# Full-array products for the state step, the key transposes and the low-rank terms, S5 outputs sorted by form, and shared raw weight buffers, in a hybrid trunk layer

## Chip, cores and metric

One Trainium2 chip, of which the kernel uses one core. The metric is device time in microseconds for one execution; the median of three runs stands for a kernel. Lower is better.

## The reference

One layer of a streaming trunk over 2128 tokens (64 of a running stream, then 16 meta tokens and 2048 of a new stream), width 1024, all in float32:

```
x  = layer_norm(x)
P  = x @ w_in                        # 1024 x 11144, columns shared out among branches and gates
y_b = branch_b(P) * silu(gate_b(P))  # b = rwkv7 (12 heads of 64), s5 (32 groups), mlstm (4 heads of 192)
m  = sum_b sigmoid(P_merge_b + b_merge_b) * (y_b @ w_br_b)
out = layer_norm(DN_ALPHA * x + m @ w_out)
```

What the change touches is mostly the rwkv7 branch. Each head keeps a 64x64 state S, and per token

```
S = S * w_t + (S @ -kk_t) (kk_t * a_t)^T + v_t k_t^T;   y_t = S @ r_t
```

where w_t and a_t come from two low-rank terms (64 columns of P times a 64 x 768 matrix each). The s5 branch is a complex diagonal recurrence with 16 channels per group. The final states of both streams are outputs too.

## The kernel before, in words

**Blocks.** The tokens go through in five blocks of 336, 448, 448, 448 and 448 columns (blocks 1 to 5 below; the first has b.first in the code). Activations lie channels on partitions, tokens along the row. A block's normalised input x stands in sixteen tiles xh0 to xh7 and xl0 to xl7: x is split into a high part (float32r) and the rest, and so is each weight. A projection of 128 columns of P (proj, L435; mm3, L427) is 24 products of 128x128 weights with a whole block of columns: high x high, high x low, low x high for eight slices of the 1024. The tiles of x have one buffer each, so a block's can be loaded (load_x, L379) only when the block before has made its last product from them.

**Weights.** In block 1 the weights come raw: split_w (L392) loads 128x512 into a raw tile, ACT copies it to the high part (L403), POOL subtracts for the low part (L404), and both parts are stored to DRAM (L409) for the later blocks, which load them ready split (L423). The table WBUF gives the numbers of buffers: three raw and four each of high and low for projections ("w"), two and two for the merge gates ("g").

**Order.** Three generators, one per branch, are mixed by weights (mix, L1449; rw_block, ml_block, s5_stream); then gate_pass (L1493) adds the block's 24 merge gates, each a projection into the PSUM tile f, behind all of the block's other work. After block 5 follow the branch outputs and the final projection (merge_pass, L1503; its products are L1556). A planner turns this program into an order per engine: it simulates a timeline and prefers what comes earlier in the program, except where high_priority says otherwise. So the gates serve as fill. All weight loads, and most other DMAs, are issued by SP's queue.

**rwkv7, one head pair at a time** (6 pairs per block). Tokens are cut into slots of 64: 6 in block 1, 7 in the others, 34 in all; two heads lie on the two halves of the partitions. rw_front (L512) makes the operands; its low-rank terms (lmm, L527 to L530) are one 128x128 product and one with 64 rows on half the array. Products of the keys with AQ are L578. rw_prep (L628) inverts the triangular part and builds per slot the transition: it transposes AQ (L625), writes an identity into AQ[:, :, 0] (POOL, L679), transposes the keys BK of each head by itself (L689), multiplies (L684, L697, L705), and adds the result to AQ (L706). rw_back (L715) runs over the slots: two products of 64x64 per slot, one for each head (called at L739, issued at L723), and one DVE operation (L741) give the next state; then come the outputs. Tiles such as XV, AR and Tt have one buffer, AQ and AT two.

**S5.** s5_block (L1310), four channel groups per block. For each of four q one weight tile of 128x512 is loaded from s5wo, then two 128x128 products from U (L1368) and eight 64x64 products from H (L1375) add into two PSUM tiles.

A float32 product appears in the trace as two records of its line, a transpose or a float32r product as one. The lines that matter, before:

```
389  WBUF = {"w": (3, 4),
530      PE.matmul(p[:, :R], lora[q, 2, :], x[q], start=False, stop=True)
689          PE.transpose(p[h][:, c, :], bk[h][:, c, :], ident[hs[h], hs[h]])
706      V.tensor_tensor(AQ[:, c0:c0 + n], AQ[:, c0:c0 + n], p[:, :n], ALU.add)
739          mm(pc[hs[h]], AQ[hs[h], c, 0, :], Ss[hs[h]], True, True)
741      V.scalar_tensor_tensor(Ss, pc, Wc[:, c:c + 1], Ss, ALU.mult, ALU.add)
```

Of the kernel before, what the change touches and what calls it, by code (L numbers as in the profile page):

```python
# [83 lines left out]
def tile_trunk(ctx: ExitStack, tc: tile.TileContext, I, O, dbg=None, parts=("rw", "s5", "ml", "mg")):  # L84
# [286 lines left out]
    G.memset(Uin, 0.0)  # L371
    Tt = pt(c1, (128, NSL, 64), "Tt")
    G.memset(Tt, 0.0)
    id2 = pt(c1, (128, 64), "id2")
    for h in range(2):
        V.tensor_copy(id2[64 * h:64 * h + 64], ident[64 * h:64 * h + 64, 64 * h:64 * h + 64])
# [15 lines left out]
    def split_w(pool, src, kt, M, tag="w", keep=None):  # L392
        if keep is not None:
            wsp_d[keep] = pt(dram, (2, 2, 128, 4, 128), f"wsp{keep}")
        nr, nh = WBUF[tag]
        hi, lo = [], []
        for k in range(0, kt, 4):
            n = min(4, kt - k)
            h = pt(pool, (128, 4, 128), tag + "hi", F32R, bufs=nh)
            l = pt(pool, (128, 4, 128), tag + "lo", F32R, bufs=nh)  # L400
            raw = pt(pool, (128, 4, 128), tag + "raw", bufs=nr)
            nc.sync.dma_start(raw[:, :n, :M], src[:, k:k + n])
            S.copy(h[:, :n, :M], raw[:, :n, :M])  # L403
            G.tensor_tensor(l[:, :n, :M], raw[:, :n, :M], h.bitcast(F32)[:, :n, :M], ALU.subtract)  # L404
            hi += [h[:, m, :M] for m in range(n)]
            lo += [l[:, m, :M] for m in range(n)]
            if keep is not None:
                for j, t in enumerate((h, l)):
                    nc.sync.dma_start(wsp_d[keep][k // 4, j], t.bitcast(F32))  # L409
        return hi, lo  # L410
# [78 lines left out]
            V.tensor_tensor(t[l, :b.R], xs[h, :b.R], t.bitcast(F32)[h, :b.R], ALU.subtract)  # L489
        return xw, xa  # L490

    lora_d = pt(dram, (NHP, 128, 384), "lora")

    def lora_setup():
        raw = flat("X", 2 * RWW)
        hl = flat("va", 2 * RWW, F32R)
        r3, h3 = (t.rearrange("p (n c) -> p n c", c=RWW) for t in (raw, hl))
        for j, w in enumerate(("rw_w2", "rw_a2")):
            for a in range(2):
                nc.sync.dma_start(r3[64 * a:64 * a + 64, j], I[w][0])  # L500
        S.copy(h3, r3)
        l = flat("NK", 770, F32R)[:, :RWW]
        for j in range(2):
            q = slice(64 * j, 64 * j + 64)
            V.tensor_tensor(l[q], r3[q, j], h3.bitcast(F32)[q, j], ALU.subtract)
        v = lora_d.rearrange("n p (j c) -> p j n c", j=3)
        f = lambda t: t.bitcast(F32).rearrange("p (n c) -> p n c", c=128)
        for j in range(2):
            nc.sync.dma_start(v[:, j], f(h3[:, j]))
        nc.sync.dma_start(v[:, 2], f(l))  # L510

    def rw_front(b, hp, xwa, cx):  # L512
        R, nc_ = b.R, b.nslot
# [7 lines left out]
        kk = pt(rp, (128, RMAX), "kk")  # L521
        V.scalar_tensor_tensor(kk[:, :R], kx[:, :R], pcol("rw_kk", hp), rn[:, :R], ALU.mult, ALU.mult)
        yield
        lora = pt(rp, (128, 3, 128), "lora", F32R)
        nc.sync.dma_start(lora.bitcast(F32).rearrange("p j c -> p (j c)"), lora_d[hp])

        def lmm(p, j):  # L527
            x, q = xwa[j][:, :R], hs[j]
            PE.matmul(p[:, :R], lora[:, j, :], x, start=True, stop=False)
            PE.matmul(p[:, :R], lora[q, 2, :], x[q], start=False, stop=True)  # L530

        pw = psum((128, 512), "tr")
        lmm(pw, 0)
# [77 lines left out]
        for j in range(31):  # L611
# [3 lines left out]
            V.tensor_tensor(t3, Uin[:, j:j + 1, j + 1:32].to_broadcast((128, m, n)),  # L615
                            Z[:, 0:m, j:j + 1].to_broadcast((128, m, n)), ALU.mult)
            V.tensor_tensor(Z[:, 0:m, j + 1:32], Z[:, 0:m, j + 1:32], t3, ALU.add)  # L617
        cx.update(AT=AT, AQ=AQ, Z=Z, ni=ni, bk=bk, Wc=Wc, vx=vx, rx=rx, sg=sg, R=R, nc_=nc_, hs=hs)
        yield

    def pair_transposes(nc_, src):
# [4 lines left out]
        return p  # L626

    def rw_prep(b, hp, cx):  # L628
        AT, AQ, Z, ni, bk, Wc, vx, rx, R, nc_, hs = (
            cx[k] for k in ("AT", "AQ", "Z", "ni", "bk", "Wc", "vx", "rx", "R", "nc_", "hs"))  # L630
        Zd = pt(dram, (8, 4, 32, 32), "Zd", bufs=2)
        for g in range(4):
            QQ.dma_start(
# [41 lines left out]
        for q in range(2):  # L675
            n = (nc_ + 1 - q) // 2
            S.copy(AR[hs[0], q:nc_:2, 0, :], p[hs[q], :n, 0:64])
            V.tensor_copy(AR[hs[1], q:nc_:2, 0, :], p[hs[q], :n, 64:128])
        G.tensor_copy(AQ[:, :nc_, 0, :], id2[:, None, :].to_broadcast((128, nc_, 64)))  # L679
        p = psum((128, 8, 64), "tr")  # L680
        for c in range(nc_):
            for h in range(2):
                o = hs[1 - h]
                PE.matmul(p[hs[h], c, :], AT[o, c, h, 0:64], XV[o, c, h, :], start=True, stop=True)  # L684
        S.copy(AR[:, :nc_, 1, :], p[:, :nc_])
        p = [psum((128, 8, 64), "tr") for _ in range(2)]
        for c in range(nc_):
            for h in range(2):
                PE.transpose(p[h][:, c, :], bk[h][:, c, :], ident[hs[h], hs[h]])  # L689
        for h in range(2):  # L690
            S.copy(AT[:, :nc_, h, 0:64], p[h][:, :nc_])
        for c0 in range(0, nc_, 4):
            n = min(4, nc_ - c0)
            p = psum((128, 4, 2, 64), "tr")
# [5 lines left out]
        for c0 in range(0, nc_, 4):  # L700
            n = min(4, nc_ - c0)
            p = psum((128, 4, 2, 64), "tr")
            for c in range(n):
                for h in range(2):
                    PE.matmul(p[hs[h], c], PX[hs[h], c0 + c, 0, :], AT[hs[h], c0 + c, h, :], start=True, stop=True)  # L705
            V.tensor_tensor(AQ[:, c0:c0 + n], AQ[:, c0:c0 + n], p[:, :n], ALU.add)  # L706
        Hw = pt(rp, (128, NSL, 64), "Hw", bufs=1)
        p = psum((128, 8, 64), "tr")
        for c in range(nc_):
# [5 lines left out]
    def rw_back(b, hp, cx):  # L715
# [14 lines left out]
        for c in range(nc_):  # L730
            with tc.high_priority(offset=HPO):
                if b.first and c == 0:
                    Ss = state_in(hp)
                elif b.first and c == 1:
                    Ss = pt(rp, (128, 64), "Ss", bufs=2)
                    G.memset(Ss, 0.0)
                S0.append(Ss)
                for h in range(2):
                    mm(pc[hs[h]], AQ[hs[h], c, 0, :], Ss[hs[h]], True, True)  # L739
                Ss = Hw[:, c, :]  # L740
                V.scalar_tensor_tensor(Ss, pc, Wc[:, c:c + 1], Ss, ALU.mult, ALU.add)  # L741
# [568 lines left out]
    def s5_block(b, u_d, y_d):  # L1310
# [3 lines left out]
        for i in range(4):  # L1314
# [45 lines left out]
            yield  # L1360
            p = [psum((128, 4, NCM), "o") for _ in range(2)]
            prev = [None, None]
            for q in range(4):
                w = cut(w5(), 0, (128, 4, 128))
                nc.sync.dma_start(w, s5wo_d[4 * i + q])
                m = []
                for g in range(2):
                    m.append((g, PE.matmul(p[g][:, q, :NC], w[:, g, :], U[:, 2 * q + g], start=True, stop=False,  # L1368
                                           skip_group_check=True)))
                for ri in range(2):  # L1370
                    for a in range(2):
                        for g in range(2):
                            r = slice(64 * g, 64 * g + 64)
                            t = slice(64 * (a ^ g), 64 * (a ^ g) + 64)
                            m.append((g, PE.matmul(p[g][t, q, :NC], w[r, 2 + ri, t], H[r, q, ri, 0:NC], start=False,  # L1375
                                                   stop=ri == 1, skip_group_check=True)))
                for g, x in m:
                    if prev[g] is not None:
                        issue_after(x, prev[g])
                    prev[g] = x  # L1380
            yS = cut(sB(), 0, (128, 8, NC))
            for g in range(2):
                S.copy(yS.rearrange("p (q g) c -> p g q c", g=2)[:, g], p[g][:, :, :NC])
# [362 lines left out]
```

## Time and profile before

| | |
|---|---|
| runs shown | 4168.24 us median of 3, 4159.67 to 4174.69 |
| profiled execution | 4180.76 us, span 4179.0 us, mean granted clock of TensorE 0.958 |
| PE, products | 3882.8 us busy (93%), 27729 records |
| PE, weight loads | 3321.6 us (79%) |
| DVE | 2513.7 us (60%) |
| ACT | 1206.4 us (29%) |
| POOL | 672.2 us (16%) |
| DMA | 834.88 MB, mean 200 GB/s |

Products overlap in the pipeline and their ends are modelled, so the distance from one start to the next tells more than a record's length. A row of the timeline holds consecutive records of one kind: start, length of the whole row, engine, line, output and inputs, shape (rows*columns of the array in use, then partitions x elements of the moving side), number of records. A half-array product shows as 64*64 or 64*128. "Busy" shares are averages over stages with different limits.

### The profile page before, as it was taken

How to read it: one execution, taken by the hardware profiler on the slowest of the kernel's cores; microseconds unless marked ns; L12 is line 12 of the kernel's file. 1: busy time of each engine (PE TensorE's matmuls, PEld its weight loads, DVE VectorE, ACT ScalarE, POOL GpSimd, SP SyncE). 2: the span in 40 equal slices, each digit the busy share in tenths (PEclk: the TensorE clock that was granted, in tenths of full speed). 3: DMA queues.
4: the chain of work that ended last, by engine and by line, in shares of the span. 5: the costliest groups of instructions: out<-in, count | busy, mean ns of one | idle time of the engine just before them, and what ended most of it. 6: DMA issues, size and time to landing. Idle time of an engine off the chain costs nothing.

```text
span 4179.0 us, 78015 instructions
## 1 busy us (share of the span) xinstructions
PE 3882.8 (93%) x27729; PEld 3321.6 (79%) x27729; DVE 2513.7 (60%) x8212; ACT 1206.4 (29%) x2655; POOL 672.2 (16%) x978
## 2 busy tenths in 40 slices
PE   6888779899999899999899999999999998999997
PEld 6777567687888788788778888778888786999997
DVE  6556887566566555656545656564666554357476
ACT  5334332233222222223222322232322232222222
POOL 5544322000000000001000001000000000232334
PEclk9999879899999899999999999999999999999999
DMA  8999647665666755666655656566565556566565
GB/s 265 314 288 313 214 132 230 181 200 184 189 212 199 238 180 182 194 186 209 190 191 176 199 184 214 174 214 204 176 204 186 158 169 183 169 197 194 160 179 161
DMA packets 803860, 834.88 MB, mean 200 GB/s; under 512 B 220246, under 2 KB 557374, under 8 KB 803470
## 3 DMA queue, kind: packets, MB, share of 16 engines
q1 hardware_dynamic: 725582, 756.61, 58.4%
q10 hardware_dynamic: 77888, 73.28, 6.0%
q8 instruction: 219, 3.59, 0.4%
q14 instruction: 171, 1.40, 0.1%
HBM read 633.92 MB, written 197.79 MB: 199 GB/s over the span
## 4 chain that ended last, share of the span: by engine, by line
PE 61%; DMA 11%; DVE 9%; SPq 2%; ACT 2%; issue 1%; POOL 1%; ACTq 0%; DVEq 0%; POOLq 0%
PE d L432 25%; PE f L432 8%; PE z L1556 7%; PE g L1556 3%; DMA xT<-X 2%; PE py L723 1%; DMA ghi<-wsp 1%; PE tr L578 1%; PE d L1411 1%; DMA E<-rd 1%; PE tr L697 1%; PE tr L705 1%; DMA Uin<-Ud 1%; PE o L1005 1%; PE o L1368 1%
## 5 line engine op out<-in xcount | busy, mean ns | idle before, releaser
L432 PE MATMUL d<-xh,whi 128*128 128x448 f32 (+1 forms) x2520 | 951.4, 378 | 31.4 <-ACT X L935 9.6
L432 PE MATMUL d<-xh,wlo 128*128 128x448 f32 (+1 forms) x2520 | 940.0, 373 | 7.5 <-POOL wlo L404 6.9
L432 PE MATMUL d<-xl,whi 128*128 128x448 f32 (+1 forms) x2520 | 933.8, 371 | 0.0
L432 PEld LDWEIGHTS d<-xh,whi 128*128 128x128 f32 x2520 | 489.1, 194 | 89.6 <-issue 14.0
L432 PEld LDWEIGHTS d<-xh,wlo 128*128 128x128 f32 x2520 | 488.3, 194 | 60.8 <-POOL wlo L404 11.2
L432 PEld LDWEIGHTS d<-xl,whi 128*128 128x128 f32 x2520 | 489.1, 194 | 44.5 <-issue 8.5
L404 POOL TENSOR_TENSOR wlo<-wraw,whi 128x512 fp32r<-128x512 f32 (+1 forms) x310 | 399.5, 1298 | 541.8 <-ACT whi L403 505.0
L432 PE MATMUL f<-xh,ghi 128*128 128x448 f32 (+1 forms) x912 | 351.2, 385 | 42.3 <-DMA ghi<-wsp 17.0
L432 PE MATMUL f<-xh,glo 128*128 128x448 f32 (+1 forms) x912 | 346.5, 380 | 14.5 <-POOL glo L404 10.3
L432 PE MATMUL f<-xl,ghi 128*128 128x448 f32 (+1 forms) x912 | 340.5, 373 | 0.0
L403 ACT CAST whi<-wraw 128x512 fp32r<-128x512 f32 (+1 forms) x310 | 179.2, 585 | 400.5 <-PE z L1556 111.5
L615 DVE TENSOR_TENSOR Ztmp<-Uin,Z 128x60 f32<-128x60 f32 (+24 forms) x930 | 214.0, 230 | 99.5 <-DMA Uin<-Ud 84.4
L432 PEld LDWEIGHTS f<-xh,ghi 128*128 128x128 f32 x912 | 180.0, 197 | 72.6 <-ACT ghi L403 18.6
L617 DVE TENSOR_TENSOR Z<-Z,Ztmp 128x60 f32<-128x60 f32 (+24 forms) x930 | 213.5, 230 | 15.6
L432 PEld LDWEIGHTS f<-xh,glo 128*128 128x128 f32 x912 | 179.6, 197 | 41.5 <-POOL glo L404 14.2
L1556 PE MATMUL z<-ya,whi 128*128 128x384 f32 (+1 forms) x784 | 192.1, 325 | 0.0
L432 PEld LDWEIGHTS f<-xl,ghi 128*128 128x128 f32 x912 | 180.5, 198 | 13.4 <-issue 2.0
L942 DVE SCALAR_TENSOR_TENSOR X<-X,PT 128x448 f32<-128x448 f32 (+1 forms) x180 | 123.0, 683 | 55.0 <-ACT X L940 53.0
L1556 PEld LDWEIGHTS z<-ya,whi 128*128 128x128 f32 x784 | 138.1, 189 | 0.2 <-issue 0.2
L1500 ACT ACTIVATE gt<-f,hbm 128x448 f32<-128x448 f32 (+1 forms) x114 | 69.9, 613 | 200.4 <-PE f L432 142.0
L1556 PE MATMUL z<-ya,wlo 128*128 128x384 f32 (+1 forms) x384 | 124.9, 325 | 0.0
L1556 PE MATMUL z<-yb,whi 128*128 128x288 f32 (+1 forms) x512 | 119.8, 316 | 2.7 <-DVE lq2i L251 1.8
(724 smaller groups left out, 6866.9 us busy)
## 6 DMA issues: line engine op xcount, KB each, us to landing
whi<-wsp SPq DMA_DIRECT2D x504, 256.0 KB
wlo<-wsp SPq DMA_DIRECT2D x504, 256.0 KB
ghi<-wsp SPq DMA_DIRECT2D x192, 256.0 KB
glo<-wsp SPq DMA_DIRECT2D x192, 256.0 KB
wraw<-in_w_in_dram SPq DMA_DIRECT2D x126, 256.0 KB
wsp<-whi SPq DMA_DIRECT2D x126, 256.0 KB
wsp<-wlo SPq DMA_DIRECT2D x126, 256.0 KB
gt<-gt SPq DMA_DIRECT2D x96, 224.0 KB
```

What stands on the lines that cost most here:

```text
L403: S.copy(h[:, :n, :M], raw[:, :n, :M])
L404: G.tensor_tensor(l[:, :n, :M], raw[:, :n, :M], h.bitcast(F32)[:, :n, :M], ALU.subtract)
L432: PE.matmul(p, a[k], c, start=i == 0, stop=i == 3 * KD - 1)
L578: i = PE.matmul(p[h][:, c].rearrange("p (j t) -> p j t", j=2), bk[h][:, c0 + c, :], AQ[hs[h], c0 + c], start=True, stop=True)
L615: V.tensor_tensor(t3, Uin[:, j:j + 1, j + 1:32].to_broadcast((128, m, n)), Z[:, 0:m, j:j + 1].to_broadcast((128, m, n)), ALU.mult)
L617: V.tensor_tensor(Z[:, 0:m, j + 1:32], Z[:, 0:m, j + 1:32], t3, ALU.add)
L697: PE.matmul(p[hs[h], c], Tt[hs[h], c0 + c, :], AR[hs[h], c0 + c], start=True, stop=True)
L705: PE.matmul(p[hs[h], c], PX[hs[h], c0 + c, 0, :], AT[hs[h], c0 + c, h, :], start=True, stop=True)
L723: i = PE.matmul(o, a, x, start=start, stop=stop, skip_group_check=True)
L942: V.scalar_tensor_tensor(acc[:, :w], raw[:, j:j + w], pcol("conv_w", 12 * j + ti), acc[:, :w], ALU.mult, ALU.add)
L1500: S.activation(t[:, :T], p[:, :T], AF.Tanh, scale=0.5, bias=hbm[:, j:j + 1])
L1556: PE.matmul(p, a[k], c[:, sl], start=i == 0, stop=i == n - 1)
```

## The change

- rw_prep no longer writes an identity into AQ[:, :, 0]. A new tile PB, zero outside its two diagonal blocks, takes the transition plus the identity, one DVE addition per head, and AQ[:, :, 1] gets an addition of its own. rw_back multiplies the whole of PB[:, c] with the state of both heads in one 128x128 product.
- The keys of both heads are transposed together, one 128x128 transpose per slot, four slots to a PSUM tile.
- The low parts of the low-rank weights get a 128x128 tile each, the unused half zero; the product takes all rows. The tile in DRAM grows from 384 to 512 columns.
- S5's output products come in two kinds: all products from U of the four q first, then all from H. A weight load takes one kind for two q, instead of both kinds for one.
- split_w takes every raw tile, those of the gates included, from the projections' three buffers.

```
+    PB = pt(c1, (128, NSL, 128), "PB")
+    G.memset(PB, 0.0)
...
-        nr, nh = WBUF[tag]
+        nh = WBUF[tag][1]
...
-            raw = pt(pool, (128, 4, 128), tag + "raw", bufs=nr)
+            raw = pt(wp, (128, 4, 128), "wraw", bufs=WBUF["w"][0])
...
-        l = flat("NK", 770, F32R)[:, :RWW]
-        for j in range(2):
-            q = slice(64 * j, 64 * j + 64)
+        ls = (flat("NK", 770, F32R)[:, :RWW],
+              pt(rp, (128, NSL, 3, 64), "XV", F32R).rearrange("p n j c -> p (n j c)")[:, :RWW])
+        for j, l in enumerate(ls):
+            q, o = slice(64 * j, 64 * j + 64), slice(64 - 64 * j, 128 - 64 * j)
+            G.memset(l.bitcast(F32)[o], 0.0)
             V.tensor_tensor(l[q], r3[q, j], h3.bitcast(F32)[q, j], ALU.subtract)
...
-            nc.sync.dma_start(v[:, j], f(h3[:, j]))
-        nc.sync.dma_start(v[:, 2], f(l))
+            nc.sync.dma_start(v[:, j], f(h3[:, j]))
+            nc.sync.dma_start(v[:, 2 + j], f(l))
...
-        lora = pt(rp, (128, 3, 128), "lora", F32R)
+        lora = pt(rp, (128, 4, 128), "lora", F32R)
...
-            PE.matmul(p[:, :R], lora[q, 2, :], x[q], start=False, stop=True)
+            PE.matmul(p[:, :R], lora[:, 2 + j, :], x, start=False, stop=True)
...
-        G.tensor_copy(AQ[:, :nc_, 0, :], id2[:, None, :].to_broadcast((128, nc_, 64)))
...
-        p = [psum((128, 8, 64), "tr") for _ in range(2)]
-        for c in range(nc_):
-            for h in range(2):
-                PE.transpose(p[h][:, c, :], bk[h][:, c, :], ident[hs[h], hs[h]])
-        for h in range(2):
-            S.copy(AT[:, :nc_, h, 0:64], p[h][:, :nc_])
+        for c0 in range(0, nc_, 4):
+            n = min(4, nc_ - c0)
+            p = psum((128, 4, 128), "tr")
+            for c in range(n):
+                PE.transpose(p[:, c], BKf[:, c0 + c, :], ident)
+            S.copy(AT[:, c0:c0 + n, :, 0:64], p[:, :n].rearrange("p c (h d) -> p c h d", h=2))
...
-            V.tensor_tensor(AQ[:, c0:c0 + n], AQ[:, c0:c0 + n], p[:, :n], ALU.add)
+            for h in range(2):
+                V.tensor_tensor(PB[hs[h], c0:c0 + n, hs[h]], p[hs[h], :n, 0],
+                                id2[hs[h], None, :].to_broadcast((64, n, 64)), ALU.add)
+            V.tensor_tensor(AQ[:, c0:c0 + n, 1, :], AQ[:, c0:c0 + n, 1, :], p[:, :n, 1], ALU.add)
...
-                for h in range(2):
-                    mm(pc[hs[h]], AQ[hs[h], c, 0, :], Ss[hs[h]], True, True)
+                mm(pc, PB[:, c, :], Ss, True, True)
...
-            for q in range(4):
-                w = cut(w5(), 0, (128, 4, 128))
-                nc.sync.dma_start(w, s5wo_d[4 * i + q])
+            for kind in range(2):
+                for q0 in (0, 2):
+                    w = cut(w5(), 0, (128, 2, 2, 128))
+                    nc.sync.dma_start(w, s5wo_d[4 * i + q0:4 * i + q0 + 2, :, 2 * kind:2 * kind + 2, :].rearrange(
+                        "q p j m -> p q j m"))
...
```

## Rows read from the trace of the kernel before

**Rows 1.** Busy time by stretch: length, PE, PEld, DVE, ACT, POOL, clock, DMA, GB/s

```profile
0.00:440.00 440.00, 360.59 (x2376) 321.07 (x2376) 260.64 (x804) 178.86 (x394) 215.75 (x274) 0.93 0.92 295
440.00:690.00 250.00, 190.07 (x1408) 150.44 (x1409) 205.95 (x870) 86.48 (x242) 72.06 (x107) 0.79 0.57 175
690.00:3420.00 2730.00, 2621.77 (x19455) 2171.27 (x19453) 1622.62 (x5640) 750.12 (x1677) 156.22 (x413) 0.97 0.62 193
```

**Rows 2.** The page's part 4, the chain that ended last, by engine

```profile
PE 61%; DMA 11%; DVE 9%; SPq 2%; ACT 2%; issue 1%; POOL 1%; ACTq 0%; DVEq 0%; POOLq 0%
```

**Rows 3.** Timeline of PE, a state step between projections (start, length, operation, records)

```profile
1734.14 0.37 PE L432 MATMUL d<-xh,whi 128*128 128x448 f32 x1
1734.35 0.37 PE L432 MATMUL d<-xl,whi 128*128 128x448 f32 x1
1734.64 0.33 PE L723 MATMUL py<-Hw,AQ 64*64 64x64 f32 x4
1734.90 0.47 PE L432 MATMUL d<-xh,wlo 128*128 128x448 f32 x1
```

**Rows 4.** Lines L723 and L741: ns min/median/max, first and last start, forms

```profile
L723 PE MATMUL py<-Hw,AQ x1344: 216/218/366, 212.2 to 3530.5; 64*64 64x64 f32 x192
...
L741 DVE SCALAR_TENSOR_TENSOR Hw<-py,Wc,Hw x204: 246/280/287, 207.4 to 3526.6; 128x64 f32<-128x64 f32 x102
```

**Rows 5.** Timeline of PE, later steps of the same head pair

```profile
1752.37 0.33 PE L723 MATMUL py<-Hw,AQ 64*64 64x64 f32 x4
1752.63 0.60 PE L578 MATMUL tr<-AQ,BK 64*128 64x128 f32 x5
...
1756.75 0.33 PE L723 MATMUL py<-Hw,AQ 64*64 64x64 f32 x4
```

**Rows 6.** Timeline of PE, two full-array float32 records before a projection

```profile
1656.87 0.32 PE L1368 MATMUL o<-sA,w 128*128 128x56 f32 x2
1657.01 0.45 PE L432 MATMUL f<-xl,ghi 128*128 128x448 f32 x1
```

**Rows 7.** Timeline of PE, a low-rank term

```profile
1018.60 0.47 PE L529 MATMUL tr<-xw,lora 128*128 128x448 f32 x1
1019.01 0.47 PE L530 MATMUL tr<-xw,lora 64*128 64x448 f32 x1
1019.41 0.47 PE L432 MATMUL d<-xh,whi 128*128 128x448 f32 x1
```

**Rows 8.** Timeline of PE, key transposes between projections

```profile
2172.94 0.36 PE L432 MATMUL d<-xh,whi 128*128 128x448 f32 x1
2173.24 0.65 PE L689 MATMUL tr<-ident,BK 64*128 64x64 f32 x7
2173.81 0.47 PE L432 MATMUL d<-xl,whi 128*128 128x448 f32 x1
```

**Rows 9.** Timeline of PE, full transposes before a projection

```profile
2519.01 1.04 PE L189 MATMUL o<-ident,X 128*128 128x128 f32 x8
2519.80 0.45 PE L432 MATMUL d<-xh,whi 128*128 128x448 f32 x1
```

**Rows 10.** Timeline of PE, S5 outputs before a projection, and between half-array products

```profile
1339.88 0.55 PE L1368 MATMUL o<-sA,w 128*128 128x56 f32 x4
1340.24 0.46 PE L432 MATMUL f<-xh,ghi 128*128 128x448 f32 x1
...
1393.64 0.65 PE L1368 MATMUL o<-sA,w 128*128 128x56 f32 x4
1394.22 0.46 PE L1375 MATMUL o<-sA,w 64*64 64x56 f32 x16
```

**Rows 11.** Line L706: ns min/median/max, first and last start, forms

```profile
L706 DVE TENSOR_TENSOR AQ<-AQ,tr x60: 415/616/690, 192.3 to 3500.5; 128x512 f32<-128x512 f32 x30, 128x384 f32<-128x384 f32 x24, 128x256 f32<-128x256 f32 x6
```

**Rows 12.** The tile graw: its loads on SP's queue, ns, first and last start

```profile
L402 SPq DMA_DIRECT2D graw<-in_w_in_dram x48: 383/455/1413, 72.0 to 424.8; - x48
```

**Rows 13.** DMA of the stretch 60 to 440 us

```profile
DMA packets 128672, 115.85 MB, mean 305 GB/s; under 512 B 17145, under 2 KB 95376, under 8 KB 128635
```

More of the change, by code (lines that the diff above doesn't have):

```diff
@@ L490, in rw_lora @@
         return xw, xa
-    lora_d = pt(dram, (NHP, 128, 384), "lora")
+    lora_d = pt(dram, (NHP, 128, 512), "lora")
     def lora_setup():
@@ L501, in lora_setup @@
         S.copy(h3, r3)
-        l = flat("NK", 770, F32R)[:, :RWW]
-        for j in range(2):
-            q = slice(64 * j, 64 * j + 64)
+        v = lora_d.rearrange("n p (j c) -> p j n c", j=4)
+        f = lambda t: t.bitcast(F32).rearrange("p (n c) -> p n c", c=128)
+        ls = (flat("NK", 770, F32R)[:, :RWW],
[3 more added lines that the diff above has]
+            G.memset(l.bitcast(F32)[o], 0.0)
             V.tensor_tensor(l[q], r3[q, j], h3.bitcast(F32)[q, j], ALU.subtract)
-        v = lora_d.rearrange("n p (j c) -> p j n c", j=3)
-        f = lambda t: t.bitcast(F32).rearrange("p (n c) -> p n c", c=128)
-        for j in range(2):
             nc.sync.dma_start(v[:, j], f(h3[:, j]))
-        nc.sync.dma_start(v[:, 2], f(l))
+            nc.sync.dma_start(v[:, 2 + j], f(l))
     def rw_front(b, hp, xwa, cx):
@@ L523, in rw_front @@
         yield
-        lora = pt(rp, (128, 3, 128), "lora", F32R)
+        lora = pt(rp, (128, 4, 128), "lora", F32R)
         nc.sync.dma_start(lora.bitcast(F32).rearrange("p j c -> p (j c)"), lora_d[hp])
         def lmm(p, j):
-            x, q = xwa[j][:, :R], hs[j]
+            x = xwa[j][:, :R]
             PE.matmul(p[:, :R], lora[:, j, :], x, start=True, stop=False)
-            PE.matmul(p[:, :R], lora[q, 2, :], x[q], start=False, stop=True)
+            PE.matmul(p[:, :R], lora[:, 2 + j, :], x, start=False, stop=True)
         pw = psum((128, 512), "tr")
@@ L617, in rw_front @@
             V.tensor_tensor(Z[:, 0:m, j + 1:32], Z[:, 0:m, j + 1:32], t3, ALU.add)
-        cx.update(AT=AT, AQ=AQ, Z=Z, ni=ni, bk=bk, Wc=Wc, vx=vx, rx=rx, sg=sg, R=R, nc_=nc_, hs=hs)
+        cx.update(AT=AT, AQ=AQ, Z=Z, ni=ni, BKf=BKf, Wc=Wc, vx=vx, rx=rx, sg=sg, R=R, nc_=nc_, hs=hs)
         yield
@@ L628, in rw_prep @@
     def rw_prep(b, hp, cx):
-        AT, AQ, Z, ni, bk, Wc, vx, rx, R, nc_, hs = (
-            cx[k] for k in ("AT", "AQ", "Z", "ni", "bk", "Wc", "vx", "rx", "R", "nc_", "hs"))
+        AT, AQ, Z, ni, BKf, Wc, vx, rx, R, nc_, hs = (
+            cx[k] for k in ("AT", "AQ", "Z", "ni", "BKf", "Wc", "vx", "rx", "R", "nc_", "hs"))
         Zd = pt(dram, (8, 4, 32, 32), "Zd", bufs=2)
@@ L1362, in s5_block @@
             prev = [None, None]
-            for q in range(4):
-                w = cut(w5(), 0, (128, 4, 128))
-                nc.sync.dma_start(w, s5wo_d[4 * i + q])
[L1366 to L1380, printed above, removed]
+            for kind in range(2):
[3 more added lines that the diff above has]
+                        "q p j m -> p q j m"))
+                    m = []
+                    for q in (q0, q0 + 1):
+                        if kind == 0:
+                            for g in range(2):
+                                m.append((g, PE.matmul(p[g][:, q, :NC], w[:, q - q0, g, :], U[:, 2 * q + g],
+                                                       start=q == 0, stop=False, skip_group_check=True)))
+                            continue
+                        for ri in range(2):
+                            for a in range(2):
+                                for g in range(2):
+                                    r = slice(64 * g, 64 * g + 64)
+                                    t = slice(64 * (a ^ g), 64 * (a ^ g) + 64)
+                                    m.append((g, PE.matmul(p[g][t, q, :NC], w[r, q - q0, ri, t], H[r, q, ri, 0:NC],
+                                                           start=False, stop=ri == 1, skip_group_check=True)))
+                    for g, x in m:
+                        if prev[g] is not None:
+                            issue_after(x, prev[g])
+                        prev[g] = x
```

## The prediction, made before the change was run

> **What bounds the kernel now.** I read the busy time by stretch first. [Rows 1] cut the run at the ends of the first block's and the last block's projections. From 690 to 3420 us, blocks 2 to 5, PE is busy 2621.8 of 2730 us (96%) at a granted clock of 0.97, while DVE is busy 59% and the DMA engines 62%: there PE's time is the kernel's time. Block 1 differs: up to 440 us the DMA engines are at 0.92 (295 GB/s) with PE at 82%; from 440 to 690 us DVE is at 82% and PE at 76%, at a clock of 0.79. The chain that ended last agrees [rows 2]: PE 61%, then DMA 11% and DVE 9%. So PE time saved in blocks 2 to 5 should come back nearly whole, and in block 1 hardly at all.
>
> Then the timeline, at the places that the diff touches. Projections of 448 columns start every 0.205 us [rows 3]. A state step between two of them is four 64x64 records (two heads, two records for each fp32 product), and the projections on its two sides start 0.55 us apart (1734.35 to 1734.90) instead of 0.205: the step costs 0.345 to 0.355. One such record lasts 0.218 us [rows 4], yet all four fit in 0.33, so the heads do run beside each other. What is dear is the edges: the first record starts 0.29 after the projection instead of 0.205, and the next projection only 0.26 after the first record.
>
> **The change part by part.**
>
> State step: 34 slots x 6 head pairs = 204 steps, as many as L741 has records [rows 4]. A step becomes one 128x128 fp32 product with 64 columns, two records. The trace has the like of it: two records of L1368 (128x128, 56 columns) between projections take 0.14 us [rows 6]. Saved where both neighbours are full array: 0.35 - 0.14 = 0.21. Where the neighbours are the 64-row key products of L578, the step takes 0.26 (first two lines of [rows 5]) and would still have an edge on either side: I take nothing saved there (a full step with both edges might lose some 0.1; the like for 40 steps is 4 us). In the timeline of the head pair at 1724 to 1757 us, four of seven steps stand between projections (first at 1734.64 in [rows 3], last at 1756.75 in [rows 5]), one stands between a low-rank term and its half-array partner, which the change makes full. I take 4.5 of 7: 131 x 0.21 = **28 us** (bounds: 10, if only a third of them count and 40 lose; 43, if all 204 count).
>
> The Trainium skill (page TensorE: Matmul & The Clock Gate, section LDWEIGHTS (loading the stationary operand)) has a weight load's time go with its columns, 107 ns for 128; by it the two loads of a full step would be 0.21 us when nothing hides them, and the saving an estimated 18 us instead of 28. [Rows 6] show the two full records in 0.14, so here the loads are mostly hidden.
>
> Low-rank terms: 60 half-array products L530. In [rows 7] L529 starts at 1018.60, L530 at 1019.01, the next projection at 1019.41: 0.81 for two products that would take 2 x 0.205 = 0.41 as full ones of the same 448 columns. That is 0.40 each; some have a cheaper first edge, so I take 0.33 x 60 = **20 us** (15 to 24). It costs one more 128x128 tile per load (256 instead of 192 KB, 30 times, 2 MB), and at the start two memsets and one more store: DMA beside other work, a microsecond or two in the full queue of the start.
>
> Key transposes: per head pair 14 records of L689 become 7 full ones. Seven of them between projections cost 0.87 - 0.205 = 0.66 us [rows 8], a pair of such runs 1.33; eight full transposes between projections cost 0.79 [rows 9], so seven about 0.69. Between the half-array products before (L684) and after (L697) the edges stay and nearly all of the gain goes. Between 0 and 0.64, I take half: 0.3 x 30 = **9 us** (0 to 19).
>
> S5 outputs: four records of L1368 cost 0.36 between projections and 0.58 between two runs of L1375 [rows 10]: 0.22 for the edges. Sorted, three of the four changes of form in each of 20 groups go: 60 x 0.22 = **13 us** (5 to 19; the planner can still put other work into the runs). Loads keep their count, 80, and their bytes; a row's piece becomes 1 KB instead of 2 KB, hidden at a DMA share of 0.62.
>
> DVE: one addition of L706 (512 elements, 0.69 us at the longest [rows 11]) becomes three of half the elements. The line's shortest, which I take for its 256-element form, is 0.415 us. As a ceiling, 3 x 0.415 - 0.69 = 0.56 us more, 60 times, 33 us of DVE, hidden in blocks 2 to 5 (DVE at 59%) and at most 6 us in block 1 if uncovered. The POOL copy into AQ goes (30, off the path). PB has one buffer where AQ had two, but its writer already waits for the output products of the pair before, through the single XV; no new wait.
>
> Sum on PE: 28 + 20 + 9 + 13 = 70 us. Blocks 2 to 5 have 28 of the 34 slots: 57 us there; PE's idle share may grow a little, so **52 us**. What is saved in block 1 I count as nothing.
>
> Raw buffers of the gates: the largest unknown. Now 48 gate loads of block 1 use two buffers of their own, from 72 to 425 us [rows 12]. After it they take turns with 126 projection loads in three. Gates come last in program order, and the planner goes by that order; I expect each freed buffer to go to a projection, so that the gates of block 1 come behind all its projections, and block 2 cannot load its xh tiles before the last gate. Moved with them: 48 loads, 96 stores of the split weights and 24 gate stores, all on SP's queue, 41.9 MB, at the 305 GB/s of 60 to 440 us [rows 13] 137 us; and 576 products of 336 columns, 0.154 each by the pace of [rows 3], 89 us of PE. In exchange the first 440 us lose up to 137 us of DMA. What is late next is DVE: 260.6 + 206.0 = 466.6 us in the first 690 [rows 1], 566 at the share of 0.82 seen after 440, which leaves room for 690 - 566 = 124. I take 100 shorter, 137 longer behind, and of the 48 us in which PE waits in that tail some 27 filled with left-over work of block 1 that now fills block 2: 137 - 100 - 27 = **10 us** lost. Bounds: 50 gained (below), 90 lost.
>
> Together 52 - 10 = 42 us less. The profiled execution took 4180.76 us (span 4179.0), 12.5 above the median of the runs shown, 4168.24; against the median I forecast 4168.24 - 42 = **4126 us**.
>
> **The rivals.**
>
> *Slower: the gates as a tail.* If block 1's rate is set by the round trips of the state branch and DVE, not by the DMA queue, its first part shrinks by only 60 us, the gates take 150 behind it, and block 1's left-overs find no room there. Then +90 - 52 = +38: 4206 us. It decides once the tail costs over 52 us more than the front wins. For it: DVE at 82% in the second part. Against: the DMA share of 0.92 in the first. Chance 0.15.
>
> *No change: the edges stay.* Fewer steps stand between full products in the new order, the planner splits the S5 runs, and only the low-rank terms count: 20 x 28/34 = 16 gained, 10 lost, 4162 us. Chance 0.15. For it: the step between L578s already costs only 0.26 [rows 5]. The Trainium skill (page TensorE: Matmul & The Clock Gate, section Part 3: Packing small matmuls) speaks for this side: small products on different tiles of the array run at once, so the packed form should be the cheap one; the trace agrees that they overlap, but shows the edges, which that section leaves out.
>
> *More: the hole in block 1 is filled.* If the gates do get buffers in between and spread over 440 to 690 us, where PE idles 60 us and the DMA engines have 0.57, block 1 ends some 50 us earlier: 4168 - 52 - 50 = 4066 us. Chance 0.15. Against: the order above.
>
> **How the numbers follow.** My own case has 0.55, with 4100 to 4155 as its own range (PE saving of 40 to 75 us, where the bounds above give 30 to 105 x 28/34 = 25 to 86; gates from 27 to 7 lost). To reach 8 in 10 the range takes in most of the gain and part of the slower case: 4058 to 4192. A measurement of this kernel can tell 0.3%, 12.5 us, from no change (runs of before lie 4159.67 to 4174.69). Faster: 0.55 + 0.15 = 0.70; within 0.3%: 0.15; slower: 0.15.
>
> **What would show it.** Right: state steps as two full-array records costing about 0.14 between projections; the products after L529 starting 0.205 apart; S5 records in long runs; PE's busy time down by 50 to 80 us and the stretch of blocks 2 to 5 about 50 us shorter than 2730. For the gates: their loads after the last projection load of block 1, at 550 us or later, and block 2 starting between 680 and 740 us. Wrong: block 2 starting after 760 us (the slower case); the stretch of blocks 2 to 5 within 15 us of now (the edges stayed, or PE's idle time took the gain); a full step that takes over 0.25 us between projections.

## The result and the profile after

The changed kernel took 4104.88 us (median of four runs, 4099.27 to 4110.26), the kernel before beside it 4163.95 us. The ratio is 0.9854, interval [0.9836, 0.9873]: 59 us less, where 42 were forecast. Set beside further runs of the kernel before, it gave 0.9863 [0.9844, 0.9883].

The profiled execution took 4099.27 us, its span 4097.5. Of the page's part 1 (busy time, share, instructions) and of part 4, the answer to [rows 2]:

```profile
PE 3785.1 (92%) x27117; PEld 3302.3 (81%) x27117; DVE 2535.4 (62%) x8332; ACT 1210.1 (30%) x2655; POOL 661.6 (16%) x951
...
PE 63%; DMA 15%; DVE 13%; SPq 3%; issue 2%; ACT 2%; POOL 1%; ACTq 0%; DVEq 0%; POOLq 0%
```

PE still bounds the kernel. Its busy time fell by 98 us (from 3882.8), DVE's rose by 22 (from 2513.7); forecast were 50 to 80 less and at most 33 more.

Where the time went is seen when the run is cut at the blocks. Block 1 here reaches to the first projection of block 2, then come block 2, blocks 3 to 5 and the merge. First the kernel before (busy time by stretch, columns as in [rows 1]):

```profile
0.00:683.00 683.00, 543.66 (x3717) 466.70 (x3717) 462.50 (x1662) 263.68 (x629) 287.81 (x381) 0.88 0.80 251
683.00:1483.00 800.00, 754.69 (x5875) 620.83 (x5876) 487.27 (x1770) 218.33 (x505) 45.64 (x120) 0.96 0.66 203
1483.00:3567.00 2084.00, 2005.47 (x14554) 1661.71 (x14550) 1203.81 (x4124) 576.18 (x1280) 112.36 (x297) 0.98 0.61 189
3567.00:4179.00 612.00, 578.98 (x3594) 572.33 (x3592) 360.14 (x657) 148.19 (x244) 226.43 (x180) 0.98 0.59 174
```

Then the changed kernel, the same stages, and the stretch of block 1's gates by itself:

```profile
0.00:776.00 776.00, 598.96 (x4445) 516.22 (x4446) 551.18 (x2075) 295.01 (x717) 289.49 (x392) 0.88 0.79 240
776.00:1458.00 682.00, 649.66 (x4708) 551.65 (x4706) 400.19 (x1384) 187.58 (x408) 41.66 (x100) 0.97 0.67 210
1458.00:3490.00 2032.00, 1958.32 (x14378) 1664.11 (x14375) 1222.95 (x4216) 578.96 (x1288) 103.45 (x279) 0.99 0.64 197
3490.00:4097.50 607.50, 578.11 (x3594) 570.35 (x3592) 361.06 (x658) 148.55 (x244) 226.99 (x180) 0.99 0.59 176
...
568.00:776.00 208.00, 174.72 (x1498) 150.88 (x1497) 107.99 (x396) 68.93 (x167) 66.27 (x65) 0.90 0.95 282
```

Block 1 became 93 us longer, block 2 118 shorter, blocks 3 to 5 52 shorter, the merge 4.5 shorter. The longer block 1 and the shorter block 2 belong together: PE runs 728 records more in the first and 1167 fewer in the second, of which the edits themselves take 126.

**The small products.** The answer to [rows 3], a state step between two projections (timeline of PE):

```profile
1495.53 0.37 PE L434 MATMUL d<-xh,whi 128*128 128x448 f32 x1
1495.73 0.33 PE L728 MATMUL py<-Hw,PB 128*128 128x64 f32 x2
1495.87 0.46 PE L434 MATMUL d<-xl,whi 128*128 128x448 f32 x1
...
1592.31 0.36 PE L532 MATMUL tr<-xw,lora 128*128 128x448 f32 x1
1592.51 0.37 PE L533 MATMUL tr<-xw,lora 128*128 128x448 f32 x1
1592.71 0.36 PE L434 MATMUL f<-xh,ghi 128*128 128x448 f32 x1
...
1572.38 0.66 PE L692 MATMUL tr<-ident,BK 128*128 128x128 f32 x4
1572.80 0.45 PE L434 MATMUL d<-xl,whi 128*128 128x448 f32 x1
...
1362.27 0.36 PE L434 MATMUL d<-xh,wlo 128*128 128x448 f32 x1
1362.56 1.15 PE L1384 MATMUL o<-sA,w 64*64 64x56 f32 x64
1363.65 0.47 PE L434 MATMUL d<-xh,whi 128*128 128x448 f32 x1
```

The projections around the step start 0.34 us apart where they were 0.55 apart; over the 85 such steps the median cost of a step is 0.138 us (0.14 was forecast). The second block answers to [rows 7]: both low-rank products now go at the pace of a projection, 0.20 each. The third answers to [rows 8]: four full key transposes, the work of eight half-array ones, 0.42 us to the next product, where seven half-array ones took 0.57. The last answers to [rows 10]: here all 64 half-array S5 records of a group stand in one run of 1.09 us; before, a run of 16 took 0.38 (1394.22 to 1394.60), four of them 1.52. That is the best case: 7 of the 20 groups got such a run, and over all groups the half-array records stand in 59 runs instead of 149.

**The raw buffers.** The answer to [rows 12] (instructions by tile, the gates' tile ghi, now split from the shared buffers; ns min/median/max, first and last start):

```profile
L405 ACT CAST ghi<-wraw x48: 601/618/652, 561.7 to 765.1; 128x512 fp32r<-128x512 f32 x48
L411 SPq DMA_DIRECT2D wsp<-ghi x48: 319/420/1004, 572.4 to 768.5; - x48
```

The gates of block 1 did go behind its projections: the first gate product starts at 567.7 us, the last projection ends at 570.4 (before: at 681.5, with the first gate product at 77.7). The stretch of the gates that follows is called the tail below.

**DVE.** The answer to [rows 11] (instructions by line):

```profile
L711 DVE TENSOR_TENSOR AQ<-AQ,tr x60: 286/388/422, 168.1 to 3434.0; 128x256 f32<-128x256 f32 x30, 128x192 f32<-128x192 f32 x24, 128x128 f32<-128x128 f32 x6
...
L709 DVE TENSOR_TENSOR PB<-tr,id x120: 275/384/428, 167.2 to 3433.6; 64x256 f32<-64x256 f32 x60, 64x192 f32<-64x192 f32 x48, 64x128 f32<-64x128 f32 x12
```

Three additions of 0.384 to 0.388 in place of one of 0.616: 0.54 more each time, as priced, and hidden in blocks 2 to 5: DVE's share there goes from 59 to 60%, and PE's idle time did not grow (124 us before, 106 after).

### The profile page after: what moved, and what is told of

The parts are those of the page before. It is cut to its first block, busy times and chain, and to the rows that moved or that the text cites. A ratio compares the mean times of both kernels' runs of the same rounds, so it can differ in the third digit from the quotient of the medians.

```text
span 4097.5 us, 77030 instructions
## 1 busy us (share of the span) xinstructions
PE 3785.1 (92%) x27117; PEld 3302.3 (81%) x27117; DVE 2535.4 (62%) x8332; ACT 1210.1 (30%) x2655; POOL 661.6 (16%) x951
## 4 chain that ended last, share of the span: by engine, by line
PE 63%; DMA 15%; DVE 13%; SPq 3%; issue 2%; ACT 2%; POOL 1%; ACTq 0%; DVEq 0%; POOLq 0%
PE d L434 28%; PE f L434 9%; PE z L1565 7%; PE g L1565 4%; DMA wraw<-in_w_in_dram 2%; PE py L728 1%; PE d L1420 1%; PE tr L581 1%; DMA xT<-X 1%; PE tr L699 1%; PE tr L707 1%; DVE Z L620 1%; DVE Ztmp L618 1%; PE o L1009 1%; DMA Uin<-Ud 1%
```

## The experiments

Every ratio is to the kernel before, run beside it (its medians: 4182.83 to 4184.58 us). Where two ratios are subtracted, 0.001 is 4.2 us.

**The raw buffers alone** (raw_alone): the kernel before with this edit and nothing else.

```
-            raw = pt(pool, (128, 4, 128), tag + "raw", bufs=nr)
+            raw = pt(wp, (128, 4, 128), "wraw", bufs=WBUF["w"][0])
```

> The kernel before with one edit of the change alone: the gates' raw weights in the projections' three buffers. Theory 'edges' (the gain is PE time that the half-array products cost at their two edges; the sharing shifts work inside block 1 and is worth about nothing): ratio to before 0.997 to 1.003; block 1's gates come behind its projections, block 2 starts 70 to 100 us later than in before, and blocks 1 and 2 together take as long as before within 15 us. Rival 'order' (the gain of the change comes from the new order of block 1, with its left-overs done beside the gates): ratio 0.991 or less, block 3 starting 30 us or more earlier than before.

Measured: 4205.90 us, 1.0044 [1.0025, 1.0062], 18 us slower. Its stretches, cut at the blocks:

```profile
0.00:793.60 793.60, 615.72 (x4531) 524.33 (x4531) 538.49 (x2050) 293.56 (x711) 292.19 (x395) 0.87 0.78 233
793.60:1505.30 711.70, 674.29 (x4978) 559.38 (x4977) 402.30 (x1381) 193.04 (x421) 42.07 (x106) 0.98 0.65 204
1505.30:3601.20 2095.90, 2019.41 (x14635) 1670.16 (x14632) 1202.26 (x4128) 581.57 (x1284) 118.45 (x297) 0.97 0.62 190
3601.20:4209.60 608.40, 578.01 (x3594) 570.82 (x3592) 354.74 (x655) 146.01 (x241) 226.49 (x180) 0.99 0.59 174
```

Block 1 is 111 us longer, block 2 88 shorter, blocks 3 to 5 are 12 longer. So the shared buffers make the tail by themselves, and on their own they lose, a little more than "edges" allowed (block 2 starts 111 us later, block 3 22) and the opposite of "order". The four edits on PE are then worth, from here to the changed kernel beside the later runs (after_again below, 0.9863), 1.0044 - 0.9863: 76 us. The ratio 0.9863 is the mark for the runs that follow.

**Each edit on PE undone, the rest of the change kept.** Four kernels, each with one part of the diff turned back. old_step: the state step as four 64x64 records, with its single DVE addition and its copy into AQ.

```
-                mm(pc, PB[:, c, :], Ss, True, True)
+                for h in range(2):
+                    mm(pc[hs[h]], AQ[hs[h], c, 0, :], Ss[hs[h]], True, True)
```

> The changed kernel with the old state step alone (two 64x64 products per slot, the identity in AQ, no PB). Edges: a step between two projections costs 0.35 us again instead of 0.14; of 204 steps about 131 count, 28 us on PE, 23 in blocks 2 to 5 and something in the rest: 23 to 30 us slower than the changed kernel, ratio to before 0.991 to 0.993. Order: within 8 us of the changed kernel, ratio 0.984 to 0.988.

Measured: 4147.60 us, 0.9907 [0.9893, 0.9921]; 18 us worse than the change, near the 23 to 30 of "edges".

old_lora: the half-array product for the low part, its tile still loaded whole.

```
-            PE.matmul(p[:, :R], lora[:, 2 + j, :], x, start=False, stop=True)
+            PE.matmul(p[:, :R], lora[q, 2 + j, :], x[q], start=False, stop=True)
```

> The changed kernel with the second low-rank product on 64 rows again (same tiles, same DMA, same number of records and columns; only the rows of the array differ). Edges: 60 products with about 0.33 us of edges each, 20 us on PE, 16 to 20 us slower than the changed kernel, ratio to before 0.989 to 0.991; the trace shows about 0.4 us from that product to the next again. Order: no difference, ratio 0.984 to 0.988.

Measured: 4174.72 us, 0.9976 [0.9964, 0.9988]; 47 us worse, where "edges" asked for 16 to 20 and "order" for none.

old_s5: the loops of the outputs by q, as before.

```
-            for kind in range(2):
-                for q0 in (0, 2):
...
+            for q in range(4):
...
```

> The changed kernel with the old order of S5's outputs (per q both kinds). Same products, same DMA bytes. Edges: 60 changes of form more at 0.22 us, 13 us on PE: 9 to 13 us slower than the changed kernel, ratio to before 0.987 to 0.989. Order: no difference, ratio 0.984 to 0.987.

Measured: 4174.23 us, 0.9975 [0.9965, 0.9986]; 47 us worse, where 9 to 13 or none were expected.

old_keys: two 64-row transposes per slot.

```
-                PE.transpose(p[:, c], BKf[:, c0 + c, :], ident)
...
+                PE.transpose(p[h][:, c, :], bk[h][:, c, :], ident[hs[h], hs[h]])
```

> The changed kernel with the keys of each head transposed by themselves again. Edges and longer streams: 9 us on PE, 0 to 19 by the bounds of the prediction, so 3 to 15 us slower than the changed kernel, ratio to before 0.986 to 0.990. Rival 'order' (what an undone part costs is mostly a worse plan, whatever is undone): 30 to 50 us slower, as for the low-rank and the S5 part, 0.993 to 0.998.

Measured: 4184.34 us, 1.0003 [0.9988, 1.0018]; 59 us worse, against 9 forecast for the edit, and beyond the 30 to 50 of the rival "order".

Together 171 us for four edits that are worth 76 as a whole. Such undoings don't measure what they seem to; the section on the prediction says what else they took.

**A step more** (step_twice): each state step's product issued twice into the same place, a known amount of work added.

```
+                mm(pc, PB[:, c, :], Ss, True, True)
                 mm(pc, PB[:, c, :], Ss, True, True)
```

> The changed kernel with each state step's product issued twice, the second writing the same result over the first: the doubled cost of a full-array step. Edges: the second product has full-array neighbours on both sides as a rule, no edge, 0.14 us, so 204 x 0.14 = 29 us on PE, 24 in blocks 2 to 5: 20 to 30 us slower than the changed kernel, ratio to before 0.990 to 0.993. Rival (a full step is dear because its 128-column weights are not hidden, 0.25 us and more): 45 us and more slower.

Measured: 4181.63 us, 1.0001 [0.9987, 1.0014], 58 us worse. Its timeline of PE at a step between projections:

```profile
1661.50 0.36 PE L434 MATMUL f<-xl,ghi 128*128 128x448 f32 x1
1661.70 0.55 PE L728 MATMUL py<-Hw,PB 128*128 128x64 f32 x4
1662.06 0.45 PE L434 MATMUL f<-xh,glo 128*128 128x448 f32 x1
```

The projections are 0.56 apart: two steps cost 0.36, so the second costs 0.22 where the first costs 0.14. 204 of them are 45 us, where 29 were expected, and 13 of the 58 are left over. Some 11 of these go with the clock, by an estimate: in blocks 2 to 5 the granted clock of TensorE, summed over the trace, stood at the lower of its two levels (1.2 GHz instead of 2.4) for 119 us, and for 94 in the changed kernel (after_again); what a microsecond there costs is shown further below.

**The changed kernel again** (after_again), run beside old_keys and step_twice.

> The changed kernel itself, beside the variants of this and the last set. If ratios carry from set to set: 0.984 to 0.988. Rival 'the day': 0.990 to 0.993, in which case undoing the low-rank or the S5 part costs 20 to 30 us and not 50.

Measured: 4126.45 us, 0.9863 [0.9844, 0.9883]. So ratios carry from set to set.

**The same work in another order.** The planner that orders the instructions answers to every edit, so I changed its input and not the work. null_swap records the addition into AQ ahead of the two into PB; null_mix and null_before change a weight of block 2's mix, in the changed kernel and in the one before.

```
+            V.tensor_tensor(AQ[:, c0:c0 + n, 1, :], AQ[:, c0:c0 + n, 1, :], p[:, :n, 1], ALU.add)
             for h in range(2):
...
-            V.tensor_tensor(AQ[:, c0:c0 + n, 1, :], AQ[:, c0:c0 + n, 1, :], p[:, :n, 1], ALU.add)
```

```
-        '0.7,1.2,2', '0.8,1.3,2', '0.8,1.3,3', '0.9,1.2,2')]
+        '0.7,1.2,2', '0.8,1.3,2.1', '0.8,1.3,3', '0.9,1.2,2')]
```

> The changed kernel with the same instructions, only the addition into AQ recorded ahead of the two into PB, so that the planner writes another order of the same work. Theory 'direct' (undoing one part cost 22 to 58 us because each part really does that much work): nothing but the order is new, ratio to the kernel before 0.984 to 0.988, as the changed kernel again (0.9863). Theory 'plan' (most of the 22 to 58 us came from writing a new order, and the order of the changed kernel is a lucky one): 15 to 45 us of it come here too, ratio 0.990 to 0.997, with more time at the lower clock level and more changes of array form than in the changed kernel.

Measured: 4157.37 us, 0.9949 [0.9927, 0.9971], 36 us worse than the changed kernel with not one record of PE more or fewer.

> The changed kernel with one weight of the mix in block 2 at 2.1 instead of 2: the same instructions in another order. Direct: ratio 0.984 to 0.988. Plan: ratio 0.990 to 0.997, the loss in blocks 2 to 5 as in the run with the addition into AQ first, though not of the same size.

Measured: 4136.11 us, 0.9888 [0.9870, 0.9905], 10 us worse; less than "plan" asked for, and not clear of the noise: the two intervals overlap.

> The kernel before with the same weight at 2.1 instead of 2. It tells how far a new order of the same work moves the kernel before. Direct: within 0.2%, ratio 0.998 to 1.002. Plan: anywhere from 0.993 to 1.007, and if it comes out faster, the order of the kernel before was a poor one and part of the 59 us is no merit of the edits.

Measured: 4178.10 us, 0.9993 [0.9979, 1.0008]: no difference that can be told.

Where null_swap lost it: block 2, then blocks 3 to 5, in the changed kernel (after_again):

```profile
786.00:1471.00 685.00, 651.43 (x4708) 552.50 (x4706) 400.20 (x1384) 187.52 (x408) 41.76 (x100) 0.97 0.67 209
1471.00:3507.00 2036.00, 1961.12 (x14377) 1666.62 (x14376) 1223.47 (x4216) 578.62 (x1288) 103.19 (x279) 0.99 0.64 197
```

and in null_swap:

```profile
790.00:1483.00 693.00, 661.81 (x4834) 561.53 (x4833) 407.70 (x1405) 190.07 (x415) 37.46 (x100) 0.98 0.68 210
1483.00:3542.70 2059.70, 1978.82 (x14250) 1670.25 (x14249) 1215.96 (x4194) 577.27 (x1279) 110.09 (x279) 0.98 0.62 193
```

32 us longer, 28 of it PE busy, at the same number of records within one: the records take longer. Two things account for part of it. The granted clock was at its lower level for 116 us instead of 94. One such stretch of after_again, with the first record after it (timeline of PE; then the busy time of the stretch):

```profile
1953.58 0.71 PE L434 MATMUL f<-xh,ghi 128*128 128x448 f32 x1 [2.64 <-DMA ghi<-wsp]
...
1956.37 0.57 PE L434 MATMUL f<-xl,ghi 128*128 128x448 f32 x1
1956.74 0.57 PE L434 MATMUL f<-xh,glo 128*128 128x448 f32 x1
...
1958.91 0.37 PE L434 MATMUL f<-xh,glo 128*128 128x448 f32 x1
1959.12 0.37 PE L434 MATMUL f<-xh,ghi 128*128 128x448 f32 x1
...
1952.00:1958.80 6.80, 5.22 (x14) 4.49 (x15) 4.88 (x21) 1.70 (x4) 0.00 (x0) 0.50 0.75 250
```

PE had waited 2.64 us for the weights of a gate; then its products start 0.373 apart instead of 0.205. All 17 such stretches in blocks 2 to 5 of after_again, and 20 of the 21 in null_swap, came behind idle time of PE. So a microsecond at the lower level costs about 0.45, and 22 of them 10 us (an estimate from these rows, as are the like figures below). And PE changed its array form 1306 times instead of 1226 (rows and columns counted as whole, half or quarter), 7 us at 0.09 each. With 4 us more of idle time, some 11 of the 32 remain without a place.

**The low-rank terms alone** (lora_alone): raw_alone with their full-array form.

```
-            PE.matmul(p[:, :R], lora[q, 2, :], x[q], start=False, stop=True)
+            PE.matmul(p[:, :R], lora[:, 2 + j, :], x, start=False, stop=True)
```

> The kernel before with the shared raw buffers and the full-array low-rank terms, nothing else; it stands against the run with the raw buffers alone (1.0044, 4206 us). By the sum of the prediction the low-rank terms are worth 15 to 24 us: ratio to the kernel before 0.999 to 1.001. Direct: they are worth the 50 us that their undoing cost, ratio 0.991 to 0.994. Plan: 15 to 24 us with the scatter that the two runs of the changed kernel in another order show.

Measured: 4191.09 us, 1.0013 [1.0001, 1.0025]: 13 us less than raw_alone (the two intervals together leave 4 to 22). Added to raw_alone, the edit is worth about what the sum gave it (its records cost 16 us less, 53 to 37); taken out of the changed kernel it seemed worth 47. Which of the two is the edit and which the order, the records themselves can say: the next section counts them.

**The gates in the mix** (gates_mixed): the changed kernel, but block 1's gates yield after each output tile and go as a fourth stream into the mix of block 1, so that they get raw buffers in between.

```
+        if b.first:
+            st.append((gate_pass(b), 2.2))
...
-        gate_pass(b)
+        if not b.first:
+            drain(gate_pass(b))
```

> The changed kernel with block 1's 24 gates given out as a fourth stream beside the three branches, so that their raw loads come in turn with the projections' instead of behind them. Theory 'tail' (the 200 us behind block 1's projections are lost to the kernel except for what left-overs fill): block 2 starts at 650 to 720 us instead of 776, the left-overs of block 1 fill block 2 again, 20 to 60 us faster than the changed kernel, ratio to before 0.972 to 0.981. Rival 'left-overs' (the tail is well used, the DMA queue sets block 1's end either way): block 2 earlier, but block 3 within 15 us of the changed kernel's, ratio 0.983 to 0.990.

Measured: 4114.66 us, 0.9832 [0.9812, 0.9851], the lowest ratio of all; its stretches:

```profile
0.00:695.40 695.40, 553.22 (x3854) 481.27 (x3854) 503.00 (x1816) 277.13 (x661) 292.70 (x386) 0.91 0.83 256
695.40:1444.70 749.30, 711.28 (x5446) 602.33 (x5446) 452.23 (x1662) 208.41 (x473) 39.80 (x106) 0.96 0.68 206
1444.70:3504.40 2059.70, 1972.89 (x14230) 1666.40 (x14230) 1212.83 (x4197) 575.08 (x1278) 105.51 (x279) 0.98 0.63 193
```

The tail is gone: block 2 starts at 695 instead of 786, ends 26 us earlier (1444.7 to 1471), and blocks 3 to 5 give 24 back (2060 against 2036), as much as in null_swap; there the clock was at its lower level for 96 us instead of 58, about 17 of the 24. The start of block 2 is as "tail" said, the ratio as "left-overs" did, and against 0.9863 the intervals overlap, so it isn't shown to be faster than the change.

Not tried: the four edits on PE with the gates' own raw buffers. What they are worth without the tail is therefore not shown.

## Why the prediction was right, and which steps were off

The time, the sign and the likeliest case came out, in part because errors offset each other: the small products saved 84 us and not 70, the raw buffers cost 18 and not 10, and the clock and the order were not in the sum at all. By its own steps:

**PE bounds blocks 2 to 5, and its gain comes back there: right, but more came than the terms.** From the stretch 690 to 3420 of [rows 1] (2730 us) to the same stretch of the changed kernel (776 to 3342, 2566 us) it is more than the 52 forecast, because left-overs of block 1 moved out of it. Blocks 3 to 5 alone gave 52. That this is the forecast figure is luck: they have 21 of the 34 slots, 43 of the 70 us. The clock helped, and the prediction had no term for it: in blocks 3 to 5 it was at its lower level for 102 us before and for 51 after, about 23 us. The fairest pair is raw_alone and after_again, which have the same tail. Blocks 2 to 5 are 87 us shorter there (2808 to 2721): by the count below some 72 from the small products, 17 from the clock (132 us at the lower level to 94) and 5 from less idle time, a little more than there is. Whether the edits or the order brought the better clock is not shown.

**The terms on PE.** I summed in the traces of before and after, for all records of a kind, the time from each start to the next product's start (short waits included), with 0.09 us for each change of form ahead of it (0.29 instead of 0.205, [rows 3]). The state step, whose neighbours matter most, I took by its neighbours:

```
                  forecast (bounds)   before   after   saved
S5 outputs            13 (5 to 19)     109       82      27
low-rank terms        20 (15 to 24)     53       31      22
key transposes         9 (0 to 19)      42       29      13
state step            28 (10 to 43)      -        -      22
sum                   70                                 84
```

In the other two orders of the changed kernel the second column of times comes out the same within 1.6 us. The first moves more: in null_before it is 116, 53 and 44, which would make the sum 92. So the edits are worth 84 to 92 us on PE in these orders, a little above the 76 between raw_alone and the changed kernel; the 171 of the undoings don't agree with either.

- *State step: the saving was right, the count was not.* A step saves 0.22 between projections (0.559 to 0.343 from start to start). But of 204 steps I had 131 between full products, from one head pair with 4.5 of 7; in the changed kernel it is 106 (of all 204, 85 stand between projections). The 53 with half-array products on both sides lost 0.10 each (0.463 to 0.566), as was said for 40. 106 x 0.22 = 23, the other 45, most with one full neighbour, x 0.10 = 5 (0.559 to 0.461 with the full one ahead), less 53 x 0.10 = 5: 22 or 23.
- *The weight load.* [Rows 6] were the right guide to a step between projections: 0.138 against the 0.21 from the Trainium skill (page TensorE: Matmul & The Clock Gate, section LDWEIGHTS (loading the stationary operand)). step_twice shows when that section's rule does come out: the second step of two costs 0.22, two loads at its 107 ns. In after_again, records in a run of full-array ones start 0.109 to 0.112 apart whether 42, 56 or 128 columns move, so this price does not go with the columns moved. That it is the weight load, hidden behind a projection for a single step and not for the next, is the likely reading; no run tests it by itself.
- *S5 outputs: mis-sized, 27 instead of 13.* The step priced the full-array runs, "60 x 0.22", and left the half-array runs at their old cost. Counted apart, the full-array records went from 53 to 41 us, which is the 12 or 13 forecast; the half-array ones went from 56 to 41, because they too stand in fewer runs (59 instead of 149).
- *Key transposes: mis-sized, 13 instead of 9.* "Between the half-array products before and after, the edges stay and nearly all of the gain goes": only 5 of the 64 runs before stood between two half-array products. The others had a full one beside them, and of the 128 changes of form at the ends of the runs 54 are left.
- *Low-rank terms: right*, 22 counted against 20 forecast, and 13 by the time of lora_alone.

**The raw buffers of the gates: the balance was near by luck, its terms were off.** 10 us lost were forecast, 18 [10, 26] came (raw_alone). In the changed kernel the front part got 111 us shorter (100 forecast; 681.5 to 570.4), and the tail took 206 us, not 137 (108 and 220 in raw_alone). At a DMA share of 0.95 the tail moved 208 us x 282 GB/s = 59 MB, of which the gates are 42; the rest belongs to the left-overs of block 1 that run there and, some 5 MB, to the first loads of block 2. The step that failed is "some 27 filled with left-over work": 922 of the stretch's 1498 PE records are not the gates' 576. PE is busy 175 us in it, and the gates' products at the forecast pace are 89, so that some 86 us (an estimate) are left-over work; block 2 became 88 us shorter in raw_alone. So the mark "wrong: block 2 starting after 760 us" was wrongly set: block 2 started at 776 us, and the loss stayed small, because what came late had made other work early. A start that slips is a loss only if the work in front of it is the same.

**The rivals.** "The gates as a tail" had the mechanism half right (a longer tail), but its front part shrank by 111 and not by 60, and the left-overs did find room. "The edges stay" fell with the 0.138 of a full step and with the changes of array form, of which the whole run has 1541 instead of 2062. "The hole in block 1 is filled" isn't what the change does; gates_mixed does it, and gained in block 1 and 2 together 26 us, not 50.

**What the prediction didn't have at all** is the order. Every edit makes the planner write a new one, and another order of the same work cost the changed kernel 36 us and, less surely, 10; the kernel before it cost nothing that can be told. So the 59 us are the edits in one order: over the three orders the mean ratio is 0.990, 42 us. That this equals the forecast is chance with three orders. By their spread a forecast for one edit of this kernel is uncertain by some 20 us beside what is known of the edit, an estimate from three orders.

What three of the undoings took beside their own records can be read from blocks 2 to 5 of their traces, against after_again, in us (records without their waits; the lower clock at 0.45 a microsecond, an estimate):

```
            longer   own records   lower clock   PE idle   not placed
old_keys      57         13             22          14          8
old_s5        43         28              2          14          0
old_lora      58         17             11          10         20
```

Their own records cost about what the count above gave them; the rest is time at the lower clock level (old_keys has 143 us of it, after_again 94) and waits. That these come from the new order and not from the edit is argued from null_swap, where the order alone brought the same kinds of loss; it is not shown.

## What to carry to other kernels

A small product costs its edges: where half-array products stand between full ones, padding them to the full array or putting them in one run is worth about 0.1 us for each change of form that goes (0.09 here), and it is counted best over all records and their neighbours, not from one example. Where a planner orders the work, an undone edit also buys another order: run the same work in two or three orders first, to know what a single comparison can tell, and look at the clock and the waits of the trace before the edit gets the whole difference. And a stage that ends later is no loss before it is seen which work went into it.

## What was not expected of the hardware

A full-array float32 product of 64 columns costs 0.14 us alone between projections, and 0.22 when it follows another one (step_twice). The same instructions of PE in another order took 28 us more of its busy time in blocks 2 to 5 (2641 instead of 2613; null_swap), part of it at the lower clock level, part of it in changes of array form; the rest stays open. A wait was often paid twice: behind PE's 2.64 us of idle time ahead of 1953.58 in after_again, its products started 0.373 us apart until 1958.6, and every stretch at the lower clock level in blocks 2 to 5 of that run came behind such a wait.
